# The second feed-forward's up products as seven block products, with weight sums made earlier and kept in DRAM

## The chip, the cores and the metric

The kernel runs on one core of one Trainium2 chip. The metric is the device time of one launch in microseconds (us), the median over runs. TensorE is called PE, its weight loads PEld, VectorE DVE, ScalarE ACT, GpSimd POOL and SyncE SP.

## The reference, cut to what matters

```python
for i in range(DEPTH):                       # two layers, 512 tokens, 256 more of context
    ...
    x = x + mods[2] * o_lat                  # layer 0: SSD and attention; layer 1: latent attention
    h = modulate(rmsnorm(x, norm2_g[i]), mods[3], mods[4])
    x = x + mods[5] * swiglu(h, ffn_w_up[i], ffn_w_down[i])
    ...
def swiglu(h, w_up, w_down):                 # w_up 1024 x 5632, w_down 2816 x 1024
    g, u = jnp.split(h @ w_up, 2, axis=-1)
    return (jax.nn.silu(g) * u) @ w_down
```

All of it is float32. In the second layer only the 512 tokens of x go through the feed-forward, in the first layer the 256 of the context too.

## The kernel before

**Numbers.** Every large product is made of three: each operand is split into a high part (rounded to fp32r) and a low part (the rest), and high x high, high x low and low x high are added up in PSUM. For a weight piece of 128 x 1024, `WStream.split` makes both parts: ACT copies the raw piece `wr` into `wh` (line 150), and POOL or DVE, by the string `W.pat`, subtracts to give `wl` (line 151). `W.lim(nraw, nhl)` sets how many raw pieces are loaded and how many split ahead; pieces come in a fixed order, and all DMAs are issued by SP's one queue (line 133 for weights).

**Stages.** The SSD and attention of layer 0 take the first 850 us or so, and then come the first feed-forward (`ffn(0, 6, ...)`, to some 1400 us), the latent attention (`mla_in`, `mla_attention`, to 1714 us), its output product with the norm of the feed-forward (`out_gemm` with `begin_norm`, to some 1787 us), the second feed-forward (`ffn(1, 4, ...)`) and the final norm. Beside the first feed-forward DVE also makes the modulation vectors (`acc`, line 409) from a stream `wa` of their own.

**A feed-forward.** The 2816 hidden columns are 11 pairs of 128-wide tiles; `FFN_PARTS` groups the pairs as 2, 3, 3, 3. Per pair there are four up pieces of 512 KB (gate and up, each in two halves of the 1024 inputs). `mm_w` (lines 662, 663, 665) keeps the weights still and moves the tokens: for each of 2 hidden tiles, gate and up, 8 input tiles and 3 forms it issues one matmul of 512 columns in the second feed-forward, 96 per pair. The first pair runs in two halves of 256 columns, so that it can begin before all tokens are normalized. `act` then makes `sg` = silu(gate) x up (ACT line 1272, DVE line 1273) and splits it into `hh` and `hl` (lines 499, 500). After each part `out_gemm` (lines 521 to 523) multiplies with the down pieces; one matmul chain per token tile and half of the outputs fills a PSUM bank `g`, of which there are two, DVE multiplies it with the gate (`gt`, line 1212), and POOL or DVE adds it to `x` (line 1213). A few steps of the next part's first up product are taken ahead of the down products.

**The attention.** 16 units, each of which ends with the row sums: DVE's reciprocal `rc`, POOL's copy `rb` (line 1068), two PE transposes, ACT's copy `rs`, DVE's product `oT`. POOL also adds the rotary parts of `q` (line 1446).

**Order.** The kernel is written as generators that are advanced side by side: `drive(main, side, ratio)` advances `side` by `ratio` steps for each step of `main`. The framework's scheduler then orders each engine's instructions once, before the run; on the chip every engine goes through its list in that order.

## Time and profile before

| | us |
|---|---|
| median of 3 runs | 2141.45 |
| lowest, highest | 2141.02, 2143.85 |
| the profiled execution | 2141.09 |
| its span | 2139.3 |

The page gives the span of one profiled execution and each engine's busy time in it; the remaining 1.8 us of its time lie around the span. Line numbers in rows are those of the kernel before. A row of a group gives busy time and mean duration of one instruction, then how long the engine had been idle just before them and what ended that. Matmuls are pipelined: their rows overlap, and the distance of two starts is what one costs.

### The profile page before, as it was taken

The page shows a single profiled execution, that of the slowest core. Times are in us where ns is not written, and L with a number is a line of the kernel's source. Part 1 is how long each engine was busy: PE and PEld are TensorE (multiplying, and loading weights), DVE is VectorE, ACT ScalarE, POOL GpSimd, SP SyncE. Part 2 cuts the span into 40 slices and gives each one's busy share as a digit, 9 for nine tenths or more (in the row PEclk, how much of TensorE's full clock was granted, in tenths as well). Part 3 has the DMA queues.
Part 4 walks back from the last instruction along what each step waited for, and adds up shares of the span by engine and source line. Part 5 has one row for each costly group of instructions (what it writes and reads, how often), then busy time and mean ns, then how long its engine had stood idle before and what let it go on. Part 6 is the DMA issues. An engine that isn't in the chain of part 4 may idle for free. (4 is left out here: it accounts for less than half of the span.)

```text
span 2139.3 us, 29481 instructions
## 1 busy us (share of the span) xinstructions
PE 2053.9 (96%) x11420; PEld 1690.0 (79%) x11420; DVE 1212.1 (57%) x2103; ACT 844.0 (39%) x1717; POOL 798.8 (37%) x701
## 2 busy tenths in 40 slices
PE   6999999999999899999999999999999999999998
PEld 3777777777777677888888878889888878888886
DVE  4689887867664697845345252175656663323223
ACT  4456544336664234312202212254655644222222
POOL 2456544584322355432222222254110154333333
PEclk9999999999999999999999999999999999999999
DMA  8211102510001641433335443112000033333232
GB/s 285 61 30 40 31 20 80 163 40 21 1 1 41 226 148 60 148 120 116 98 105 163 148 129 97 52 51 53 15 12 31 30 94 104 90 99 100 87 98 69
DMA packets 127573, 179.52 MB, mean 84 GB/s; under 512 B 16189, under 2 KB 77770, under 8 KB 127434
## 3 DMA queue, kind: packets, MB, share of 16 engines
q1 hardware_dynamic: 127434, 177.64, 26.4%
q8 instruction: 90, 1.47, 0.3%
q14 instruction: 49, 0.40, 0.1%
HBM read 172.35 MB, written 5.27 MB: 83 GB/s over the span
## 5 line engine op out<-in xcount | busy, mean ns | idle before, releaser
L151 POOL TENSOR_TENSOR wl<-wr,wh 128x1024 fp32r<-128x1024 f32 (+3 forms) x125 | 304.1, 2434 | 403.0 <-ACT wh L150 291.7
L150 ACT ACTIVATE wh<-wr 128x1024 fp32r<-128x1024 f32 (+3 forms) x211 | 218.6, 1038 | 520.0 <-DMA wr<-in_ffn_w_up_dram 135.5
L663 PE MATMUL gu<-hl,wh 128*128 128x512 f32 (+1 forms) x768 | 288.2, 376 | 1.5 <-POOL hl L500 1.5
L662 PE MATMUL gu<-hh,wh 128*128 128x512 f32 (+1 forms) x768 | 288.4, 376 | 0.0
L665 PE MATMUL gu<-hh,wl 128*128 128x512 f32 (+1 forms) x768 | 287.6, 375 | 0.0
L409 DVE SCALAR_TENSOR_TENSOR acc<-wa,sst,acc 128x512 f32<-128x512 f32 (+1 forms) x196 | 183.1, 977 | 89.1 <-DMA wa<-in_ada_w_dram 89.0
L151 DVE TENSOR_TENSOR wl<-wr,wh 128x1024 fp32r<-128x1024 f32 (+3 forms) x86 | 115.1, 1338 | 167.2 <-ACT wh L150 143.9
L521 PE MATMUL g<-wh,hh 128*128 128x512 f32 (+2 forms) x520 | 199.4, 384 | 0.5 <-DVE gt L1212 0.5
L522 PE MATMUL g<-wl,hh 128*128 128x512 f32 (+2 forms) x520 | 198.3, 381 | 0.0
L523 PE MATMUL g<-wh,hl 128*128 128x512 f32 (+2 forms) x520 | 197.4, 381 | 0.0
L1212 DVE TENSOR_TENSOR gt<-g,gate 128x512 f32<-128x512 f32 x132 | 90.5, 689 | 180.0 <-PE g L523 176.6
L662 PEld LDWEIGHTS gu<-hh,wh 128*128 128x128 f32 x768 | 144.4, 188 | 30.3 <-issue 2.9
L500 POOL TENSOR_TENSOR hl<-sg,hh 128x768 fp32r<-128x768 f32 (+1 forms) x44 | 71.8, 1632 | 247.0 <-ACT hh L499 246.9
L663 PEld LDWEIGHTS gu<-hl,wh 128*128 128x128 f32 x768 | 144.7, 188 | 16.6 <-POOL hl L500 1.7
L665 PEld LDWEIGHTS gu<-hh,wl 128*128 128x128 f32 x768 | 144.7, 189 | 15.6
L1052 DVE TENSOR_REDUCE nm<-S 128x1 f32<-128x768 f32 x128 | 122.1, 954 | 48.4 <-PE S L1512 27.6
L1213 POOL TENSOR_TENSOR x<-x,gt 128x512 f32<-128x512 f32 x66 | 89.6, 1362 | 131.6 <-DVE gt L1212 122.8
L248 PE MATMUL PTp<-ident,Pm 128*128 128x128 f32 x832 | 123.1, 276 | 6.5 <-ACT PT L1087 2.1
L1054 ACT ACTIVATE Pm<-S,nm 128x768 f32<-128x768 f32 x128 | 115.1, 899 | 25.2 <-DVE nm L1052 24.4
L248 PEld LDWEIGHTS PTp<-ident,Pm 128*128 128x128 f32 x832 | 96.0, 141 | 23.5 <-issue 9.2
L521 PEld LDWEIGHTS g<-wh,hh 128*128 128x128 f32 x520 | 97.6, 188 | 20.0 <-DVE gt L1212 1.0
L523 PEld LDWEIGHTS g<-wh,hl 128*128 128x128 f32 x520 | 97.7, 188 | 19.5
(311 smaller groups left out, 4687.2 us busy)
## 6 DMA issues: line engine op xcount, KB each, us to landing
wa<-in_ada_w_dram SPq DMA_DIRECT2D x96, 512.0 KB, 4.8
wr<-in_ffn_w_up_dram SPq DMA_DIRECT2D x88, 512.0 KB, 3.6
wr<-in_ffn_w_down_dram SPq DMA_DIRECT2D x44, 512.0 KB, 4.2
wr<-in_ab_w_in_dram SPq DMA_DIRECT2D x36, 512.0 KB, 3.8
wr<-in_ab_w_out_dram SPq DMA_DIRECT2D x16, 512.0 KB, 5.5
wr<-in_mla_w_o_dram SPq DMA_DIRECT2D x8, 512.0 KB, 3.6
yscr<-y SPq DMA_DIRECT2D x12, 256.0 KB, 3.7
yr<-yscr SPq DMA_DIRECT2D x6, 512.0 KB, 4.2
```

The lines of the kernel that those rows point to most:

```text
L150: nc.scalar.activation(hi, raw, AF.Copy)
L151: eng.tensor_tensor(lo, raw, r32(hi), op=ALU.subtract)
L248: self.nc.tensor.transpose(out, in_, self.ident[:n, :n])
L409: nc.vector.scalar_tensor_tensor(acc[:, v], in0=raw[:, kk], scalar=c, in1=acc[:, v], op0=ALU.mult, op1=ALU.add)
L521: nc.tensor.matmul(ps, h, wh[:, kk, :], start=(n == 0), stop=False)
L522: nc.tensor.matmul(ps, h, wl[:, kk, :], start=False, stop=False)
L523: nc.tensor.matmul(ps, l, wh[:, kk, :], start=False, stop=(n == nk - 1))
L662: nc.tensor.matmul(o, a, hi[:, c0:c1], start=st, stop=False)
L663: nc.tensor.matmul(o, a, lo[:, c0:c1], start=False, stop=False)
L665: nc.tensor.matmul(o, b, hi[:, c0:c1], start=False, stop=sp)
L1052: nc.vector.tensor_reduce(nm, sp[:, :, 0:w], axis=AX.XY, op=ALU.max, negate=True)
L1054: nc.scalar.activation(p[:, 0:nkt * P].rearrange("p (a b) -> p a b", a=2), sp[:, :, 0:w], AF.Exp, bias=nm, accum_out=x["sum"][:, ti, a:a + 1])
```

## The change

The feed-forward of layer 1 is rewritten for pairs 1 to 10. The tokens (two halves of 256) and the inputs (two halves of 512) cut the activations into four blocks `11`, `12`, `21`, `22`; the inputs, and gate and up, cut a pair's weights into four. The two-by-two block product, which takes eight block products, is made with seven, of which four use sums of weight blocks and four use sums of activation blocks (`S1` to `S4`). Each block product is 24 matmuls of 256 columns (`mm_q`). `up7` adds up the results out of PSUM: five sums on DVE, two copies on ACT, two sums on POOL, then Silu, products and splits.

The sums of weights are made by `sums_w`, four per block, from a second load of the weights (`wq`), and stored to a DRAM tile `w7` that the weight stream reads later: pairs 1 to 5 on DVE beside the first feed-forward (40 items of 128x128 blocks), pairs 6 to 10 on POOL beside the attention (20 items of 128x256). An item is two loads, four operations and one store. A pair takes seven pieces of 512 KB instead of four; four of them are read from `w7`. `begin_norm_q` keeps the normalized tokens (`hfT`), and `sums_q` makes the activation sums between the halves of the first pair, eight DVE operations and their splits. All of a part's hidden tiles of a pair come out of the last of its products; one product of the next part is taken ahead of the down products. In the attention and the output product all weight splits go to DVE, in the second feed-forward two of three (`VVP`); four raw pieces are loaded and five split ahead there. The modulation vectors of layer 1 get one or two steps more between their product and its use.

```diff
+SUMS_0, SUMS_1, SUMS_2 = 6, 0.16, 0.17
...
+def along(main, side, ratio, wait):
+    acc = -wait * ratio
+    for _ in main:
+        acc += ratio
+        while acc >= 1.0:
+            acc -= 1.0
+            next(side, None)
+        yield
+    for _ in side:
+        pass
...
             for j in pairs:
-                gs = bp(up, 0, KD, 256 * j, 256, 4)
-                self.i_up[l, j] = (pre + W.add(gs[len(pre):]), W.add(bp(up, 0, KD, HID + 256 * j, 256, 4)))
+                ops = self.up_pieces(l, j)
+                ids = pre + [W.add([s])[0] for s in ops[len(pre):]]
+                self.i_up[l, j] = (ids[:2], ids[2:]) if len(ids) == 4 else ids
...
+    def up_pieces(self, l, j):
+        up = self.a["ffn_w_up"][l]
+        g, u = (self.block_pieces(up, 0, KD, x + 256 * j, 256, 4) for x in (0, HID))
+        if l == 0 or j == 0:
+            return g + u
+        if j not in self.w7:
+            self.w7[j] = self.dp.tile([P, 4, 4, 256], F32, name=self.nm("w7"))
+        t = [self.w7[j][:, n] for n in range(4)]
+        return [g[0], t[1], t[0], g[1], t[3], t[2], u[1]]
+
+    def sums_w(self, pairs, w, V, alloc):
+        nc = self.nc
+        up = self.a["ffn_w_up"][1].rearrange("(s k p) (x f) -> k s p x f", s=2, p=P, x=2)
+        items = [(j, kt, c) for j in pairs for kt in range(4) for c in range(0, 256, w)]
+        def load(j, kt, c):
+            t = alloc([P, 2, 2, w], F32, "wq")
+            for s in range(2):
+                nc.sync.dma_start(t[:, s], up[kt, s][:, :, 256 * j + c:256 * j + c + w])
+            return t
+        ts = [load(*x) for x in items[:2]]
+        yield
+        for n, (j, kt, c) in enumerate(items):
+            t = ts.pop(0)
+            V.tensor_tensor(t[:, 0, 1], t[:, 1, 1], t[:, 0, 1], op=ALU.subtract)
+            V.tensor_tensor(t[:, 0, 0], t[:, 0, 0], t[:, 0, 1], op=ALU.add)
+            yield
+            V.tensor_tensor(t[:, 1, 0], t[:, 1, 0], t[:, 0, 0], op=ALU.subtract)
+            V.tensor_tensor(t[:, 1, 1], t[:, 1, 1], t[:, 0, 0], op=ALU.subtract)
+            yield
+            if n + 2 < len(items):
+                ts.append(load(*items[n + 2]))
+            nc.sync.dma_start(self.w7[j][:, :, kt, c:c + w], t.rearrange("p s x c -> p (s x) c"))
+            t = None
...
+    def split_q(self, src, name, tt, eng):
+        c = slice(tt * P, tt * P + P)
+        (h3, h1), (l3, l1) = self.q[name]
+        for h, lo, s in ((h3[:, :, c], l3[:, :, c], src[:, 0:3]), (h1[:, c], l1[:, c], src[:, 3])):
+            self.nc.scalar.activation(h, s, AF.Copy)
+            eng.tensor_tensor(lo, s, r32(h), op=ALU.subtract)
...
+    def sums_q(self):
+        V, G = self.nc.vector, self.nc.gpsimd
+        self.quarters(("S1", "S2", "S3"))
+        for tt in range(2):
+            h1, h2 = self.hf[tt], self.hf[2 + tt]
+            a11, a12, a21, a22 = h1[:, 0:4], h1[:, 4:8], h2[:, 0:4], h2[:, 4:8]
+            V.tensor_tensor(a22, a21, a22, op=ALU.add)
+            V.tensor_tensor(a21, a11, a21, op=ALU.subtract)
+            self.split_q(a21, "S3", tt, G)
+            V.tensor_tensor(a11, a22, a11, op=ALU.subtract)
+            self.split_q(a11, "S2", tt, V)
+            self.split_q(a22, "S1", tt, G)
+            V.tensor_tensor(a12, a12, a11, op=ALU.subtract)
+            self.split_q(a12, "S4", tt, V)
...
+    def mm_q(self, outs, i, name, start, stop):
...
+        for o, m0 in outs:
+            for kk in range(4):
...
+                nc.tensor.matmul(o, a, hi, start=st, stop=False)
+                nc.tensor.matmul(o, a, lo, start=False, stop=False)
+                nc.tensor.matmul(o, b, hi, start=False, stop=sp)
...
+    def up7(self, ids, hh, hl):
...
+            elif n == 2:
+                t["u2"] = two(self.med(512, "hf"))
+                V.tensor_tensor(t["u2"], ps, t["p1"], op=ALU.add)
+            elif n == 3:
+                sg = t["sg"] = self.e([P, 2, 2, 256], F32, "sg7")
+                V.tensor_tensor(sg[:, :, 0], ps, t.pop("p1"), op=ALU.add)
+                nc.scalar.activation(sg[:, :, 0], sg[:, :, 0], AF.Silu)
+            elif n == 4:
+                w, u2 = t["w"], t["u2"]
+                V.tensor_tensor(w[:, 0], ps, u2, op=ALU.add)
+                G.tensor_tensor(u2, u2, w[:, 1], op=ALU.add)
+                G.tensor_tensor(w[:, 1], w[:, 1], w[:, 0], op=ALU.add)
...
+        for n, name in enumerate(("11", "S3", "S2", "12", "S1", "22", "S4")):
...
+            yield from self.mm_q([(ps[:, m], m * P) for m in range(2)], ids[n], name, True, True)
+            self.W.free(ids[n])
+            ev(n, ps)
+            yield
...
-        drive(self.ffn(0, NT, LateGates(self, 0, 5, side), lambda: self.begin_norm(1, 0)), side, ADA_DVE)
+        drive(along(self.ffn(0, NT, LateGates(self, 0, 5, side), lambda: self.begin_norm(1, 0)),
+                    self.sums_w(range(1, SUMS_0), P, nc.vector, self.s), SUMS_1, 60), side, ADA_DVE)
...
-        drive(self.mla_attention())
+        W.pat = "V"
+        W.lim(2, 3)
+        drive(along(self.mla_attention(), self.sums_w(range(SUMS_0, 11), 256, nc.gpsimd, self.f), SUMS_2, 2))
...
-        drive(self.out_gemm(self.oh, self.ol, 4, self.i_mo[1], range(NL), gate, self.begin_norm(1, 3)))
+        W.lim(2, 4)
+        drive(self.out_gemm(self.oh, self.ol, 4, self.i_mo[1], range(NL), gate, self.begin_norm_q(1, 3)))
...
-        W.lim(1, 6)
+        W.pat = "VVP"
+        W.lim(4, 5)
         gate = [self.gate(1, 5, 0)]
-        drive(self.ffn(1, NL, gate, self.final))
+        drive(self.ffn_q(1, gate, self.final))
```

**The order, first place: POOL in the second attention.** Before, between two units' copies `rb`, stand rotary sums (`q`) or nothing:

```order
L1446 TENSOR_TENSOR q_13734<-q_13734,qp_13890 128x4x32
L1068 COPY rb_13929<-rc_13927 128x256
L1068 COPY rb_14054<-rc_14052 128x256
L1068 COPY rb_14180<-rc_14178 128x256
L151 TENSOR_TENSOR wl_14216<-wr_13878,wh_14215 128x768
L1068 COPY rb_14381<-rc_14379 128x256
```

With the change, the additions of the weight sums (`wq`) are among them:

```order
L1123 COPY rb_14100<-rc_14098 128x256
L1677 TENSOR_TENSOR q_14077<-q_14077,qp_14117 128x4x32
L636 TENSOR_TENSOR wq_14155<-wq_14155 128x256
L637 TENSOR_TENSOR wq_14155<-wq_14155 128x256
L1677 TENSOR_TENSOR q_14077<-q_14077,qp_14150 128x4x32
L639 TENSOR_TENSOR wq_14155<-wq_14155 128x256
L640 TENSOR_TENSOR wq_14155<-wq_14155 128x256
L1677 TENSOR_TENSOR q_14078<-q_14078,qp_14196 128x4x32
L1677 TENSOR_TENSOR q_14078<-q_14078,qp_14247 128x4x32
L1123 COPY rb_14292<-rc_14290 128x256
```

Every item puts four additions on POOL, and a weight split (`wl`) no longer stands there.

**Second place: DVE at the end of the first part of the first feed-forward.** Before, the gated products `gt` of the down product follow each other:

```order
L1273 TENSOR_TENSOR sg_9050<-sg_9050,gu_8919 128x512
L1276 TENSOR_TENSOR sg_9050<-sg_9050,gc_8920 128x256
L409 SCALAR_TENSOR_TENSOR acc_8927<-wa_9105,sst_76,acc_8927 128x512 x4
L1212 TENSOR_TENSOR gt_9100<-g_9087,gate_9101 128x512
L1212 TENSOR_TENSOR gt_9122<-g_9109,gate_9101 128x512
L1212 TENSOR_TENSOR gt_9140<-g_9125,gate_9101 128x512
```

Now eleven additions stand ahead of these rows and eight more between the first three products:

```order
L639 TENSOR_TENSOR wq_9279<-wq_9279 128x128
L1267 TENSOR_TENSOR gt_9158<-g_9145,gate_9159 128x512
L640 TENSOR_TENSOR wq_9279<-wq_9279 128x128
L1267 TENSOR_TENSOR gt_9182<-g_9167,gate_9159 128x512
L637 TENSOR_TENSOR wq_9348<-wq_9348 128x128
L639 TENSOR_TENSOR wq_9348<-wq_9348 128x128
L640 TENSOR_TENSOR wq_9348<-wq_9348 128x128
L636 TENSOR_TENSOR wq_9426<-wq_9426 128x128
L637 TENSOR_TENSOR wq_9426<-wq_9426 128x128
L639 TENSOR_TENSOR wq_9426<-wq_9426 128x128
L640 TENSOR_TENSOR wq_9426<-wq_9426 128x128
L1267 TENSOR_TENSOR gt_9200<-g_9185,gate_9159 128x512
```

At the ends of the second and third part the additions stand in the same way, up to 28 ahead of the third `gt`.

**Third place: DVE within a pair of the second feed-forward.** Before, a pair is two products `sg` and two weight splits:

```order
L1273 TENSOR_TENSOR sg_17182<-sg_17182,gu_17109 128x512
L151 TENSOR_TENSOR wl_17171<-wr_17144,wh_17170 128x1024
L1273 TENSOR_TENSOR sg_17238<-sg_17238,gu_17189 128x512
L151 TENSOR_TENSOR wl_17271<-wr_17180,wh_17270 128x1024
```

Now it is five sums out of PSUM (`gu`, `gc`), a product, a split `hl` and four or five weight splits:

```order
L1480 TENSOR_TENSOR hf_18236<-gu_18205,hf_18170 128x512
L165 TENSOR_TENSOR wl_18231<-wr_18093,wh_18230 128x1024
L1487 TENSOR_TENSOR w_18203<-gu_18271,hf_18236 128x512
L1483 TENSOR_TENSOR sg_18268<-gu_18205,hf_18170 128x2x256
L165 TENSOR_TENSOR wl_18297<-wr_18168,wh_18296 128x1024
L1492 TENSOR_TENSOR sg_18268<-gu_18271,hf_18236 128x2x256
L165 TENSOR_TENSOR wl_18330<-wr_18201,wh_18329 128x1024
L1497 TENSOR_TENSOR w_18203<-gc_18338,w_18203 128x512
L1498 TENSOR_TENSOR sg_18268<-sg_18268,w_18203 128x2x256
L516 TENSOR_TENSOR hl_18376<-sg_18268,hh_18375 128x512
```

The weight splits stand between the sums that free PSUM.

## Rows read from the trace of the kernel before

**Rows 1.** Page, part 1: busy time, share of the span, instructions by engine.
```profile
PE 2053.9 (96%) x11420; PEld 1690.0 (79%) x11420; DVE 1212.1 (57%) x2103; ACT 844.0 (39%) x1717; POOL 798.8 (37%) x701
```

**Rows 2.** Stretches: first feed-forward, attention, output product, second feed-forward.
```profile
core 0: us, PE busy (x) PEld busy (x) DVE busy (x) ACT busy (x) POOL busy (x), PEclk, DMA share, GB/s
850.00:1400.00 550.00, 546.21 (x3005) 463.30 (x3004) 247.95 (x342) 124.38 (x186) 164.84 (x97) 0.99 0.37 116
1490.00:1714.00 224.00, 216.30 (x1536) 189.58 (x1534) 141.50 (x234) 133.10 (x283) 26.86 (x38) 0.99 0.07 22
1714.00:1787.00 73.00, 71.16 (x417) 62.33 (x418) 45.11 (x85) 32.64 (x68) 37.32 (x35) 1.00 0.31 97
1787.00:2101.00 314.00, 314.00 (x1358) 254.69 (x1358) 83.12 (x86) 85.83 (x100) 111.85 (x62) 1.00 0.32 97
```

**Rows 3.** Waits of PE, 840 to 1400 us, then 1720 to 2140: total, times, longest.
```profile
PE ada L419 <- DVE acc L409: 2.7, 1, 2.7
...
PE gu L663 <- POOL hl L500: 1.5, 1, 1.5
```

**Rows 4.** Timeline of PE (92 matmuls, first and last) and of its weight loads.
```profile
1776.08 0.28 PE L662 MATMUL gu<-hh,wh 128*128 128x256 f32 x1
...
1786.83 0.28 PE L665 MATMUL gu<-hh,wl 128*128 128x256 f32 x1
...
1776.44 0.19 PEld L663 LDWEIGHTS gu<-hl,wh 128*128 128x128 f32 x1
1776.56 0.19 PEld L665 LDWEIGHTS gu<-hh,wl 128*128 128x128 f32 x1
```

**Rows 5.** Groups by form in the second feed-forward, 1787 to 2101 us.
```profile
L151 POOL TENSOR_TENSOR wl<-wr,wh 128x1024 fp32r<-128x1024 f32 x29 | 69.6, 2399 | 96.4 <-ACT wh L150 87.4 <-PE g L523 9.0
L150 ACT ACTIVATE wh<-wr 128x1024 fp32r<-128x1024 f32 x58 | 61.5, 1061 | 175.9 <-DMA wr<-in_ffn_w_up_dram 116.5 <-DMA wr<-in_ffn_w_down_dram 34.9 <-POOL wl L151 24.5
...
L151 DVE TENSOR_TENSOR wl<-wr,wh 128x1024 fp32r<-128x1024 f32 x29 | 41.9, 1444 | 77.4 <-ACT wh L150 64.4 <-PE gu L663 12.5 <-PE g L522 0.5
...
L1273 DVE TENSOR_TENSOR sg<-sg,gu 128x512 f32<-128x512 f32 x21 | 14.5, 688 | 80.2 <-ACT sg L1272 80.2
```

**Rows 6.** Line 151, the low split: ns min/median/max of DVE's.
```profile
L151 DVE TENSOR_TENSOR wl<-wr,wh x86: 559/1226/2343, 286.4 to 2097.6; 128x1024 fp32r<-128x1024 f32 x79, 128x768 fp32r<-128x768 f32 x4, 128x384 fp32r<-128x384 f32 x2, 128x864 fp32r<-128x864 f32 x1
```

**Rows 7.** Timeline, 1826 to 1830 us: start, length, engine.
```profile
1826.85 1.29 POOL L1213 TENSOR_TENSOR x<-x,gt 128x512 f32<-128x512 f32 x1 [5.61 <-DVE gt L1212]
...
1827.23 1.99 DVE L151 TENSOR_TENSOR wl<-wr,wh 128x1024 fp32r<-128x1024 f32 x1 [0.46 <-PE g L522]
...
1829.15 0.68 DVE L1212 TENSOR_TENSOR gt<-g,gate 128x512 f32<-128x512 f32 x1
```

**Rows 8.** DMA issues in the second feed-forward: count, KB, us to landing.
```profile
wr<-in_ffn_w_up_dram SPq DMA_DIRECT2D x35, 512.0 KB, 3.6
```

**Rows 9.** Groups by form of DVE in the first feed-forward.
```profile
L409 DVE SCALAR_TENSOR_TENSOR acc<-wa,sst,acc 128x1024 f32<-128x1024 f32 x28 | 37.1, 1323 | 53.1 <-DMA wa<-in_ada_w_dram 53.0
...
L500 DVE TENSOR_TENSOR hl<-hf,hh 128x128 fp32r<-128x128 f32 x17 | 7.1, 452 | 0.0
```

**Rows 10.** Waits of SP's queue, 840 to 1450 us: total, times, longest.
```profile
SPq L133 <- PE g L523: 168.9, 17, 47.5
```

**Rows 11.** Line 1164, a 128x256 subtraction on POOL: ns min/median/max.
```profile
L1164 POOL TENSOR_TENSOR ol<-of,oh x24: 725/737/1050, 509.6 to 692.4; 128x256 fp32r<-128x256 f32 x24
```

**Rows 12.** Tile rb in the second attention: first and last start.
```profile
L248 PE MATMUL O<-ident,rb x32: 270/272/299, 1518.5 to 1709.0; 128*128 128x128 f32 x32
L1068 POOL COPY rb<-rc x16: 397/402/407, 1504.4 to 1705.6; 128x256 f32<-128x256 f32 x16
```

**Rows 13.** Groups by form, 1714 to 1787 us: the weight splits.
```profile
L151 POOL TENSOR_TENSOR wl<-wr,wh 128x1024 fp32r<-128x1024 f32 x6 | 15.2, 2538 | 5.0 <-ACT wh L150 2.9 <-DVE wl L151 1.8 <-POOL hl L500 0.2
...
L151 DVE TENSOR_TENSOR wl<-wr,wh 128x1024 fp32r<-128x1024 f32 x6 | 7.3, 1220 | 8.8 <-PE gu L663 6.5 <-ACT wh L150 2.3
```

More of the change, by code (lines that the diff above doesn't have):

```diff
@@ new lines, in begin_norm_q, with norm, after @@
+    def begin_norm_q(self, l, ch):
+        nc = self.nc
+        self.q, self.hf = {}, [None] * NL
+        self.quarters(("11", "12", "22"))
+        self.quarters(("21", "S4"))
+        A, B = self.mod[l][:, ch + 1, 0, :], self.mod[l][:, ch, 0, :]
+        live = {}
+        def norm(xn, t):
+            hf = self.hf[t] = self.e([P, KD, P], F32, "hfT")
+            for h in range(2):
+                ps = self.ps("nT", [P, 4, P])
+                for i in range(4):
+                    kt = 4 * h + i
+                    self.tr(ps[:, i, :], xn[:, kt * P:(kt + 1) * P])
+                for i in range(4):
+                    kt = 4 * h + i
+                    nc.vector.tensor_scalar(hf[:, kt, :], ps[:, i, :], A[:, kt:kt + 1], B[:, kt:kt + 1], op0=ALU.mult, op1=ALU.add)
+                self.split_q(hf[:, 4 * h:4 * h + 4], f"{t // 2 + 1}{h + 1}", t % 2, nc.gpsimd if h else nc.vector)
+        def after(t, nb):
+            if nb == 0:
+                live[t] = self.f([P, D], F32, "xn"), self.small(2, "s2")
+            xn, s2 = live[t]
+            self.norm_half(self.x[t], xn, s2, nb)
+            if nb == 0:
+                return None
+            del live[t]
+            nc.scalar.activation(xn, self.x[t], AF.Copy, scale=self.rstd2(s2))
+            return lambda: norm(xn, t)
+        return after
```

96 lines of the change are left out of this document (91 added, 5 removed).

## The prediction

> **What bounds the kernel now.** I read the page first, then the stretches, then the waits of TensorE, then single rows. PE is busy 96% of the span [rows 1]. [...]
>
> **Term 1, the matmuls: minus 23.7 us.** A pair of hidden tiles (j = 1 to 10) now takes 96 matmuls of 512 columns; the change makes seven products of 24 matmuls of 256 columns, 168 in all. The 512-column step is 314.00 / 1358 = 0.2312 us [rows 2]. The 256-column step stands in the first pair, which already runs in halves: from 1776.08 to 1786.83 us there are 92 matmuls, so 10.75 / 91 = 0.118 us [rows 4]. That is a little over half of 0.2312, so halving the columns loses only some 2%. Per pair: 96 x 0.2312 = 22.20 us against 168 x 0.118 = 19.82 us, 2.37 us less; ten pairs give 23.7 us. The first pair keeps its 192 matmuls of 256 columns, and the down products are unchanged.
>
> A narrow matmul could be held up by its own weights: each step loads a new 128x128 block, one load is 0.19 us in the rows, longer than the 0.118 us step, and loads too start every 0.12 us [rows 4]. They overlap, so the step above is already the price with a load each time. [...]
>
> **Term 2, engines beside the second feed-forward: plus 5 us.** Per pair the weight pieces go from four to seven. Each costs ACT 1.06 us, then POOL 2.40 us or DVE 1.23 us undisturbed [rows 5, 6]. By the pattern VVP that is 4.67 x 1.23 = 5.7 us on DVE, 2.33 x 2.40 = 5.6 us on POOL and 7.4 us on ACT. The seven products add five DVE sums out of PSUM at 0.69 us (the price of the sg product [rows 5]), 3.4 us, and on DVE a multiply and a split with both inputs in SBUF, 0.69 us each, 1.4 us; POOL gets two sums, a product and one split at some 1.3 us (its 128x512 sum takes 1.29 [rows 7]), 5.2 us; ACT two copies, two Silus and two splits at about 0.6 us, 3.7 us. Sums: DVE 10.5, POOL 10.8, ACT 11.1 us, each under 19.8 us.
>
> What speaks against adding these up apart: DVE and POOL disturb each other. A DVE split takes 1226 ns in the median and up to 2343; one that starts at 1827.23 us, inside a POOL sum that ends at 1828.14 us, takes 1.99 us, about what it has to wait plus its usual time, while the DVE product from PSUM beside the next POOL work keeps its length [rows 5 to 7]. If DVE's 7.1 us of two-SBUF-input work and POOL's 10.8 us exclude each other, that is 17.9 us of 19.8 us per pair: it fits with 10% to spare. If every POOL instruction fully delays DVE, DVE needs 10.5 + 10.8 = 21.3 us, 1.5 us too much per pair. Bounds for ten pairs: 0 and 15 us; I take 4, nearer the lower end, because five pieces are split ahead (four products, 11 us of PE work) and DVE's PSUM sums can run beside POOL. [...]
>
> The last product of a part leaves a DVE sum, a DVE multiply, two ACT splits and two low splits before the down products: 0.69 + 0.69 + 1.3 + 1.3 = 4.0 us. PE has the first 12 down matmuls (2.8 us) and, except in the last part, one product taken ahead (2.8 us) as cover: 0 to 1.2 us at the last, 1 us taken.
>
> Traffic is no term: seven pieces of 0.52 MB in 19.8 us are 185 GB/s against 97 GB/s now at a 0.32 share of the DMA engines [rows 2], so about 0.6, and a piece lands in 3.6 us [rows 8] where it is loaded four ahead.
>
> **Term 3, the sums in the first feed-forward: plus 2 us.** DVE gets 160 additions of 128x128 beside 248 us of work in 550 us [rows 2]. A DVE operation of that shape with two SBUF inputs is 452 ns here, contention included [rows 9], so about 72 us; from the 0.69 us of four times the columns at least 28 us. DVE goes to 60% at most. What matters is who stands behind them: in the order, 20 to 28 additions stand ahead of the third gated product (gt) of each of three parts, and a late gt holds one of two PSUM banks of the down products. PE takes 12 x 0.231 = 2.8 us per bank in the first part, 18 x 0.231 = 4.2 us later. At 452 ns 20 additions (first part) are 9.0 us and 28 are 12.7 us; three banks of cover are 8.3 and 12.5 us. So 0 to 1 us per part if the loads have landed; 2 us taken, from 0 to 10.
>
> On SP the sums issue 80 loads and 40 stores in the same queue as the weights, and a store heads the queue until DVE has done its four additions. The queue has room: it waits 168.9 us for PE to release buffers [rows 10], so the weights are ahead of their use.
>
> **Term 4, the sums in the second attention: plus 1.5 us.** POOL gets 80 additions of 128x256 at 737 ns [rows 11], 59 us beside 27 us of work in 224 us [rows 2]. Behind them on POOL stand the 16 copies rb, on which each unit's last step hangs. Between two of them the order shows four to eight additions, so a copy may come up to 5.9 us later. In the trace the first copy is at 1504.4 and its product on PE at 1518.5 us, the last 3.3 us ahead at 1705.6 and 1709.0 us [rows 12]: mostly slack. Bounds 0 and 8 us.
>
> **Term 5, between attention and second feed-forward: plus 2.5 us.** From 1714 to 1787 us POOL made six weight splits (15.2 us) and DVE six (7.3 us) [rows 13]; now DVE makes all of the output product's, beside 45 us of work in 73 [rows 2]. The activation sums add eight DVE operations of 0.69 us or more, and splits on DVE and POOL; they are due one after the other over the first pair's second half and the next products, some 16 to 30 us. Bounds 0 and 8 us; PE waited 1.5 us here before.
>
> **The sum.** 2141.09 us (the profiled execution, 0.36 us under the median of the runs) - 23.7 + 4 + 1 + 2 + 1.5 + 2.5 = 2128.4 us. I forecast **2128.5 us**.
>
> **The rivals.**
> - *All covered.* Every added operation hides: 2141.1 - 23.7 = 2117.4 us. For it: PE has next to no waits anywhere now [rows 3], with the same kind of stream. Against: four places where a margin is only some microseconds.
> - *DVE and POOL saturate.* Each POOL instruction delays DVE in full, 15 us in term 2 instead of 4: 2139.4 us, no measurable change. For it: the 1.99 us row; against: DVE's PSUM sums need no turn. [...]
> - *Late products in the first feed-forward (slower).* The additions wait for their own loads: DVE goes through two items in a burst, and if one landing of 3.6 us [rows 8] is open for every two of six items, 10.8 us come on top of, say, 24 x 0.452 = 10.8 us. The third gt is then some 10 us late, in three parts 30 us: 2128.4 + 28 = 2156 us. It decides as soon as loads are issued behind stores that wait; below about 3 us of lateness per part nothing shows. Against: DVE waits 53 us for the loads of one form of acc in this stretch [rows 9], and PE does not notice.
> - *Weights not overlapped.* If each 256-column step took the 0.19 us of its load [rows 4], a pair would take 168 x 0.19 = 31.9 us, 9.7 more than now: 97 us for ten pairs, 2238 us. Against: the 92 matmuls at 0.118 us. [...]
> - *The change does not do what it says.* Were the sums not finished in their stages, a block of them would stand before the next stage. The order has the last four of DVE's in the last part's first pair and the last of POOL's ahead of the last o splits, so I give this no share.
>
> **How the numbers follow.** Between runs of this kernel 0.2% (4.3 us) is about what can be told from no change. Forecast 0.58 (2121 to 2137 us), all covered 0.16, saturated 0.12, late products 0.10, weights 0.01, something not listed on the slower side 0.03. Faster: the first two and a sixth of the saturated case, 0.76; the same: the rest of the saturated and a little of the late case, 0.11; slower 0.13. The range runs from 2117 us, the covered case, to 2144 us, past the saturated case and into the first of the late one; some 0.15 is left out. The forecast's own range is 2121 to 2137 us.
>
> **What would show it.** Right: matmuls of the second feed-forward at 0.118 us, its stretch about 20 us shorter, PE's waits there a few microseconds on DVE and POOL splits. Term 2 is wrong if PE waits for wl pieces in every pair, with DVE splits near 2 us. Term 3 is wrong if PE waits for gt between 860 and 1390 us, term 4 if it waits for rs in attention. The forecast falls if the 256-column step is not 0.118 us, or if the stretches before 1714 us grow by more than 10 us.

## The result, and the profile after

The change takes **2121.25 us** (median of 5 runs, 2119.75 to 2125.81) against 2142.07 us for the kernel before in the same comparison: a ratio of 0.9907, with an interval of 0.9893 to 0.9921. That is 20 us less, 17 to 23 by the interval; forecast were 2128.5 us, 12.6 us less than the profiled execution of before. The profiled execution of the change took 2120.97 us, its span 2119.2 us. Medians and ratios here and below are over the runs in the faster state, which leaves out one of the four runs of e3 (7582.58 us).

The page's first part, to be held against [rows 1], and three stretches, to be held against [rows 2] (same columns; the last is cut to where the change's own stage lies):

```profile
PE 2036.3 (96%) x12140; PEld 1710.1 (81%) x12140; DVE 1369.5 (65%) x2361; ACT 890.5 (42%) x1770; POOL 886.6 (42%) x791
```

```profile
850.00:1400.00 550.00, 544.86 (x2977) 459.49 (x2976) 291.21 (x492) 122.95 (x181) 161.78 (x95) 0.99 0.48 151
1490.00:1712.00 222.00, 217.10 (x1537) 190.15 (x1536) 143.89 (x237) 134.63 (x284) 74.94 (x113) 0.98 0.37 115
1788.00:2078.00 290.00, 286.85 (x2041) 269.02 (x2040) 173.28 (x169) 125.76 (x152) 152.70 (x82) 0.99 0.50 155
```

PE has 720 instructions more and 17.6 us less work. In the second feed-forward it made 1358 matmuls in 314 us; now 2041 in 290. DVE has there 173 us of work in 290, POOL 153, ACT 126: the busy share of DVE has more than doubled, and PE still has 99%.

To see where the 20 us lie, the span is cut at the first and last starts of three kinds of matmul: the scores `S` of the second attention, the last form of the output product (`ol`) and of the down products (`hl`). First the kernel before, then the change (ns min/median/max, first and last start, forms):

```profile
L1510 PE MATMUL S<-kb,mQ x128: 331/340/522, 1490.8 to 1701.8; 96*128 96x384 f32 x128
...
L523 PE MATMUL g<-wh,ol x160: 387/393/628, 677.5 to 1760.5; 128*128 128x512 f32 x160
...
L523 PE MATMUL g<-wh,hl x520: 292/392/405, 932.8 to 2131.1; 128*128 128x512 f32 x147, 128*128 128x288 f32 x16, 128*128 128x384 f32 x11
```

```profile
L1741 PE MATMUL S<-kb,mQ x128: 333/338/446, 1491.3 to 1700.5; 96*128 96x384 f32 x128
...
L539 PE MATMUL g<-wh,ol x160: 387/394/628, 671.1 to 1758.9; 128*128 128x512 f32 x160
...
L539 PE MATMUL g<-wh,hl x520: 292/394/501, 929.9 to 2111.1; 128*128 128x512 f32 x147, 128*128 128x288 f32 x16, 128*128 128x384 f32 x11
```

The differences of these starts, for the two and for the kernels of the experiments (us; "attention" is from the first to the last `S`, "output" from there to the last `ol`, "second FFN" from there to the last `hl`):

| | to the first S | attention | output | second FFN | rest | span |
|---|---|---|---|---|---|---|
| before | 1490.8 | 211.0 | 58.7 | 370.6 | 8.2 | 2139.3 |
| the change | 1491.3 | 209.2 | 58.4 | 352.2 | 8.1 | 2119.2 |
| e1 products alone | 1487.7 | 202.9 | 58.5 | 352.0 | 8.1 | 2109.2 |
| e2 sums alone | 1489.4 | 209.3 | 58.8 | 371.6 | 7.9 | 2137.0 |
| e3 first bank | 1493.4 | 209.0 | 58.4 | 351.6 | 8.1 | 2120.5 |
| e4 pattern VP | 1493.8 | 209.6 | 58.4 | 353.6 | 8.1 | 2123.5 |
| e5 before, three ahead | 1488.2 | 203.8 | 58.7 | 370.5 | 8.2 | 2129.4 |
| e6 before, splits on DVE | 1488.9 | 210.0 | 58.7 | 370.5 | 9.1 | 2137.2 |
| e7 own buffers | 1488.5 | 203.9 | 58.5 | 352.5 | 8.1 | 2111.5 |
| e8 all splits on POOL | 1491.5 | 209.9 | 58.4 | 393.6 | 8.1 | 2161.5 |
| e9 buffers and bank | 1490.8 | 205.5 | 58.4 | 351.7 | 8.1 | 2114.5 |
| e10 all sums on DVE | 1515.4 | 203.1 | 58.4 | 350.8 | 8.2 | 2135.9 |
| e11 all sums on POOL | 1490.6 | 236.3 | 58.4 | 350.7 | 8.2 | 2144.2 |
| e12 three edits | 1492.2 | 205.5 | 58.4 | 351.5 | 8.1 | 2115.7 |

Two things stand in the first two lines. The second feed-forward gives 18.4 us, not the 23.7 of the matmuls alone. And the attention, where the change adds 59 us of POOL work, is 1.8 us *shorter*. The first column moves by 5 us between kernels that do the same work there (1488.5 in e7, 1493.8 in e4), so a few microseconds of any one execution are not the change's. The attention column holds such a piece too: in most executions the granted clock drops as the attention begins (to a mean of 0.96 over 40 us in e9, against 1.00 in e7), in e1, e5, e7, e10 and e11 it does not, and that is worth 1.6 us (the last section has the rows). The medians and their intervals carry the totals, the stages carry the reasons.

What PE waits for in the change (total, times, longest), first in the first feed-forward, then in the attention, then from the output product to the end:

```profile
PE g L537 <- DVE gt L1267: 1.7, 3, 0.9
...
PE PTp L262 <- DVE PT L1140: 1.9, 1, 1.9
...
PE g L1695 <- ACT PT L1142: 0.4, 1, 0.4
...
PE gu L1458 <- DVE sg L1540: 3.1, 1, 3.1
PE gu L1459 <- DVE q L1396: 0.6, 1, 0.6
```

Against [rows 3], and the same wait of the kernel before,

```profile
PE g L521 <- DVE gt L1212: 0.5, 1, 0.5
```

there is one new wait of 3.1 us at the entry of the second feed-forward, there are waits for `gt` in the first feed-forward of 1.7 us instead of 0.5, and two for `PT` in the attention. After 1794 us PE waits for nothing at all.

### The profile page after: what moved, and what is told of

Its sections match the earlier page's. It is cut to its first block, busy times and chain, and to the rows that moved or that the text cites. A ratio compares the mean times of both kernels' runs of the same rounds, so it can differ in the third digit from the quotient of the medians.

```text
span 2119.2 us, 31924 instructions
## 1 busy us (share of the span) xinstructions
PE 2036.3 (96%) x12140; PEld 1710.1 (81%) x12140; DVE 1369.5 (65%) x2361; ACT 890.5 (42%) x1770; POOL 886.6 (42%) x791
## 4 chain that ended last, share of the span: by engine, by line
PE 75%; DVE 12%; DMA 4%; ACT 4%; issue 3%; POOL 2%; SPq 0%; POOLq 0%; DVEq 0%; ACTq 0%
PE g L537 9%; PE g L538 8%; PE g L539 8%; PE O L1154 4%; PE PTp L262 4%; PE gu L717 3%; PE gu L718 3%; PE gu L720 3%; DVE acc L423 3%; PE gu L1459 2%; PE gu L1458 2%; PE gu L1460 2%; PE S L1223 2%; DMA wa<-in_ada_w_dram 2%; PE gc L720 2%
## 5 line engine op out<-in xcount | busy, mean ns | idle before, releaser
L164 ACT ACTIVATE wh<-wr 128x1024 fp32r<-128x1024 f32 (+3 forms) x241 | 250.0, 1040 | 483.1 <-PE g L538 181.9
L165 POOL TENSOR_TENSOR wl<-wr,wh 128x1024 fp32r<-128x1024 f32 (+2 forms) x115 | 286.0, 2488 | 361.7 <-ACT wh L164 233.3
L165 DVE TENSOR_TENSOR wl<-wr,wh 128x1024 fp32r<-128x1024 f32 (+3 forms) x126 | 174.6, 1386 | 79.3 <-ACT wh L164 65.0
L717 PE MATMUL gu<-hh,wh 128*128 128x512 f32 (+1 forms) x384 | 145.1, 378 | 0.0
L718 PE MATMUL gu<-hl,wh 128*128 128x512 f32 (+1 forms) x384 | 144.9, 377 | 0.0
L720 PE MATMUL gu<-hh,wl 128*128 128x512 f32 (+1 forms) x384 | 144.6, 377 | 0.0
L516 POOL TENSOR_TENSOR hl<-sg,hh 128x768 fp32r<-128x768 f32 (+1 forms) x34 | 62.4, 1837 | 165.3 <-ACT hh L515 152.4
L538 PEld LDWEIGHTS g<-wl,hh 128*128 128x128 f32 x520 | 98.5, 189 | 17.9
L537 PE MATMUL g<-wh,h1h 128*128 128x512 f32 x240 | 97.7, 408 | 3.9 <-DVE zt L968 3.9
L718 PE MATMUL gc<-hl,wh 128*128 128x256 f32 x352 | 99.0, 281 | 0.0
```

The lines of the kernel that those rows point to most:

```text
L164: nc.scalar.activation(hi, raw, AF.Copy)
L165: eng.tensor_tensor(lo, raw, r32(hi), op=ALU.subtract)
L537: nc.tensor.matmul(ps, h, wh[:, kk, :], start=(n == 0), stop=False)
L538: nc.tensor.matmul(ps, h, wl[:, kk, :], start=False, stop=False)
L717: nc.tensor.matmul(o, a, hi[:, c0:c1], start=st, stop=False)
L718: nc.tensor.matmul(o, a, lo[:, c0:c1], start=False, stop=False)
```

## The experiments

Ratios are to the kernel before on the same chip, with 95% intervals. Most intervals are 0.3% (6 us) wide, so single-microsecond questions are answered by the stage table and the waits.

**Which part costs, which gains: the products alone, the sums alone.** e1 reads all seven pieces of a pair from the weights and makes no sums:

```diff
-        if j not in self.w7:
-            self.w7[j] = self.dp.tile([P, 4, 4, 256], F32, name=self.nm("w7"))
-        t = [self.w7[j][:, n] for n in range(4)]
+        t = g + u
...
-        drive(along(self.mla_attention(), self.sums_w(range(SUMS_0, 11), 256, nc.gpsimd, self.f), SUMS_2, 2))
+        drive(self.mla_attention())
```

> Left out: the weight sums (their loads, additions and stores); the four pieces of a pair that were read from the sums' tile are read from the weights themselves, so that traffic, splits, products and activation sums are those of the change. By the prediction the sums cost 2 us in the first feed-forward and 1.5 us in the attention: this kernel is then 3.5 us faster than the change, near 2118. If the sums are covered (the trace of the change shows PE waiting 1.7 us for gt in the first feed-forward and next to nothing for POOL in the attention), it lies within 1.5 us of the change, 2119.5 to 2121. If the late products were at work after all, it gains 10 us or more.

Measured: 2113.0 us, 0.9867 (0.9853 to 0.9881), 28.5 us less than before. Against the change's 0.9907 the sums cost 0.40%, 8.6 us (the two intervals allow 3 to 15): more than the forecast's 3.5. The table puts 6.3 us of it in the attention (202.9 against 209.2; 4.7 without the clock drop at its start) and 3.6 ahead of it, which is within what that column moves by anyway. And it shows something that none of the expectations had: without sums the attention is 8.1 us shorter than *before*, 6.5 without the clock drop. Whatever that is, it is part of the change, and it isn't the products.

e2 is the other half, the sums with the old second feed-forward (`up_pieces` returns `g + u` for all pairs, `begin_norm` and `ffn` as before):

> The sums are made and stored as in the change, with the attention's splits on DVE, but the second feed-forward is the one of before and does not read them. By the prediction: 3.5 us over before, near 2145.5. If the sums are covered: within 2 us of before, 2142 to 2144. If late gated products cost as the slower rival has it: 15 to 28 us over before, 2157 to 2170.

Measured: 2138.15 us, 0.9984 (0.9975 to 0.9993), 3.4 us less than before: a kernel with 240 more additions, 120 loads and 60 stores that isn't slower at all. The late gated products as a heavy cost are out at this size. That it is faster points again to the attention (209.3 against 211.0).

**The hidden gain: three pieces split ahead.** With the sums the change sets `W.pat = "V"` and `W.lim(2, 3)` for the attention; before it was `PV` and `lim(2, 2)`. e5 is the kernel before with the limit alone, e6 with the pattern alone:

```diff
+        W.lim(2, 3)
         drive(self.mla_attention())
```

> The kernel before with one edit: in the second attention three weight pieces are split ahead instead of two, still in turn on POOL and DVE; no sums, the old second feed-forward. The ledger of the traces gives the change 6.3 us there which the prediction's sum does not hold: PE's five waits for the query weights' splits (4.7 us by rows, with the slower restart behind them) are gone. If it is the number split ahead: those waits vanish here, 5 to 6.5 us faster than before, near 2135. If it is the engine (DVE in place of POOL): no change here, 2140 to 2141.

> The kernel before with the other half of that edit: in the second attention all weight splits on DVE, still two ahead. If the number split ahead is the cause: PE's waits for wh stay (3.4 us) and only those for POOL's wl (1.3 us) go, 0 to 2 us faster, 2138.5 to 2140.5. If the engine is the cause: 5 to 6.5 us faster, near 2135.

Measured: e5 2133.48 us, 0.9973 (0.9963 to 0.9983); e6 2138.26 us, 0.9998 (0.9988 to 1.0008). The limit does it, 5.8 us by the ratio, 7.2 by the table (203.8 against 211.0), or 5.6 without the clock drop, which stands ahead of the first of these waits (in the kernel before the mean granted clock is 0.83 from 1490 to 1500 us, and the first wait for `wh` ends at 1507.30) and so is not the limit's; the engine does nothing that can be told from no change. PE's waits in the attention, of the kernel before and of e6 (same columns as above):

```profile
PE g L521 <- ACT wh L150: 3.4, 3, 1.2
PE g L522 <- POOL wl L151: 1.3, 2, 0.6
```

```profile
PE g L521 <- ACT wh L150: 3.4, 3, 1.2
```

The three waits for `wh` stay in e6 and are gone in e5 and in the change. They are the first of the query weights (`cqT` products), split too late because only two split pieces may live at a time; ACT makes the copy in 0.51 us once the place is free, then POOL the low part in 1.0 us, and PE stands there. So one line of the change, which does not belong to the seven products, is worth about a quarter of what they are. A kernel with that line alone is the right one to compare the products with: by ratio 2133.5 to 2121.25 is 12 to 14 us, not 20.

**What the sums cost in the attention: buffers, not work.** In the change ACT, DVE and PE come to a stop once, around 1632 us. The timeline of the change (start, length, engine, and in brackets the idle time before it and what ended it):

```profile
1628.01 0.56 SPq L644 DMA_DIRECT2D w<-wq  x1
...
1631.90 0.60 ACT L1142 ACTIVATE PT<-PTp 128x512 f32<-128x512 f32 x1 [3.80 <-DMA w<-wq]
1632.39 1.05 ACT L164 ACTIVATE wh<-wr 128x1024 fp32r<-128x1024 f32 x1
...
1632.55 0.44 PE L1695 MATMUL g<-cvT,wh 128*128 128x384 f32 x1 [0.42 <-ACT PT L1142]
...
1633.48 1.64 DVE L165 TENSOR_TENSOR wl<-wr,wh 128x1024 fp32r<-128x1024 f32 x1 [3.16 <-ACT wh L164]
...
1635.03 0.68 DVE L1140 COPY PT<-PTp 128x512 f32<-128x512 f32 x1
```

The store of a finished item is issued at 1628.01; ACT's copy `PT` has waited 3.80 us for it to land. `PT` and the sums' tiles `wq` come from one pool of 14 buffers, so the next `PT` takes over a buffer that a sum still holds. Behind ACT's copy, in its fixed order, stands the split `wh`; DVE waits 3.16 us for that, its own copy `PT` is late, PE waits 0.42 and 1.90 us. e7 gives the sums tiles from the pool that holds the residual `x`:

```diff
-        drive(along(self.mla_attention(), self.sums_w(range(SUMS_0, 11), 256, nc.gpsimd, self.f), SUMS_2, 2))
+        drive(along(self.mla_attention(), self.sums_w(range(SUMS_0, 11), 256, nc.gpsimd, self.e), SUMS_2, 2))
```

> The change with one edit: the second attention's weight sums take their tiles from the pool of the residual x, not from the one that also holds the copies PT and the weight pieces. In the change's trace ACT stands 3.80 us at a copy PT until a store of the sums has landed, DVE's next weight split waits 3.16 us for ACT, and PE waits 0.4 and 1.9 us for PT; a clock drop of 3.4 us follows. If the shared buffers are the cause: those waits are gone, 2.5 to 4.5 us faster than the change, 2116 to 2118. If it is POOL's additions as such (59 us of work, the prediction's reason), nothing changes, 2120 to 2121.5.

Measured: 2117.99 us, 0.9899 (0.9882 to 0.9915); the interval overlaps the change's, the stage is clearer: the attention goes from 209.2 to 203.9 us, 1.0 above e1, which makes no sums there. Of these 5.3 us, 1.6 are the clock drop at its start; e9 and e12, which have the same attention and the drop, take 205.5 us. So the buffers are worth some 3.7 us. POOL does the same 80 additions. PE's waits for `PT` in e7:

```profile
PE PTp L262 <- DVE PT L1140: 0.7, 2, 0.4
```

**How far each engine's slack goes.** e10 puts all sums on DVE (`SUMS_0, SUMS_1 = 11, 0.32`), e11 all on POOL (`SUMS_0, SUMS_2 = 1, 0.34`, with e7's pool).

> All ten pairs' weight sums on DVE beside the first feed-forward, 320 additions of 291 ns (93 us) at twice the rate, none on POOL. Up to 56 additions then stand ahead of a third gt: 16.3 us against 12.5 us of cover. If the late gated product is only off in size (the slower rival's mechanism): 3.8 us in each of three parts, 11 us more in the first feed-forward, less 4.5 us gained in the attention: near 2127. If the additions keep to DVE's idle time: 1.2 us of gt waits become 2 to 3, the attention gains 2.8 to 4.5: 2117 to 2119.

> All ten pairs' weight sums on POOL in the second attention, 160 additions of 731 ns (117 us beside 27 in 222), with tiles from the pool of x, none on DVE. If POOL's work is idle-time work once the buffers are its own: the first feed-forward gains 2.6 us over the run with own buffers and the attention loses under 1 us: 2115 to 2117. If the additions ahead of the copies rb begin to tell (up to 16 of 0.73 us, 11.7 us, against the 3.3 us of slack at the last copy): 8 us for the last units, 2124 or more; the sums' loads (40 of 0.26 MB more) are then also behind the weights on SP.

Measured: e10 2139.34 us, 1.0008 (0.9997 to 1.0020); e11 2144.64 us, 1.0029 (1.0019 to 1.0040). Each loses the whole gain. In e10 the stretch up to the first `S` is 24 us longer than in the change, and PE's waits between 840 and 1440 us say where it starts:

```profile
PE g L537 <- DVE gt L1267: 10.2, 7, 4.1
...
PE ada L433 <- DVE gt L1267: 1.9, 1, 1.9
PE g L538 <- DVE wl L165: 1.8, 1, 1.8
```

The `gt` waits, 1.7 us in the change, are 10.2 us, with 1.9 more where a modulation product follows, and splits and `hh` behind them. The expectation of 11 us for that mechanism had its size for these waits. From 840 us to the first `S` all of PE's waits together are some 17 us longer than in the change; the rest of the 24 us is not taken apart here. So the slower rival is real; the change stays below the load at which it costs much, by a factor of less than two.

e11 fell neither way that was written down: the attention is 27 us longer than in the change, and what PE waits for is not the copies `rb`. Its waits between 1480 and 1740 us, of PE, then of ACT and DVE:

```profile
PE PTp L262 <- DVE mQ L1723: 18.3, 3, 7.7
...
ACT mQ L1722 <- DMA w<-wq: 26.2, 5, 9.6
...
DVE mQ L1723 <- DMA w<-wq: 15.8, 2, 11.2
```

ACT and DVE wait 26.2 and 15.8 us for stores of sums before they may write `mQ`, which comes from the pool of `x` too. By the trace that is e7's mechanism again, in the other pool: at twice the rate of items the stores hold more buffers than are free. No run gives these sums more buffers, so this is read from the waits and not tested. Whether POOL itself has room for all sums isn't shown by this run.

**Whether POOL and DVE get in each other's way.** In the second feed-forward every other split on POOL (e4, `"VP"`), and all of them (e8, `"P"`):

> In the second feed-forward every other weight split goes to POOL instead of every third. Per pair of 19.84 us POOL then has 3.5 x 2.40 + 5.2 = 13.6 us and DVE 3.5 x 1.23 + 4.8 = 9.1 us by undisturbed durations. If each POOL instruction delays DVE in full (the saturated rival), DVE needs 22.7 us a pair: 2.9 us more than PE, some 29 us over the change, 2150. If only DVE's instructions with two SBUF inputs exclude POOL (5.7 us of the 9.1), 19.3 us: it just fits, 0 to 8 us slower, 2121 to 2129. If the two engines hardly disturb each other: no change, 2120 to 2122.

> In the second feed-forward all weight splits on POOL: 7 x 2.40 + 5.2 = 22.0 us of POOL work per pair of 19.84 us by undisturbed durations. If POOL's sum alone decides: 2.2 us over PE in each of ten pairs, some 22 us over the change, 2142, less what is made up during the down products (five pieces ahead, at most 3 parts x 5 x 2.4 us). If DVE's instructions with two SBUF inputs also hold POOL (1.4 us a pair): 2150 to 2156. If the work ahead covers it: 2121 to 2126.

Measured: e4 2123.37 us, 0.9916 (0.9902 to 0.9929); e8 2164.16 us, 1.0128 (1.0103 to 1.0153). e4 lies in the range of the middle theory and 26 us below full delay; its interval overlaps the change's, so it does not tell the middle theory from no disturbance. e8 is past the point where POOL alone decides. Its second feed-forward (same columns as the stretches above):

```profile
1788.00:2078.00 290.00, 267.27 (x1795) 244.81 (x1794) 100.32 (x100) 111.00 (x132) 245.32 (x124) 0.96 0.44 136
```

POOL is at 245 of 290 us there, PE at a granted clock of 0.96, and the stage takes 41.4 us more than in the change, above every expectation. PE's waits from 1788 us on come to 29.7 us, against 3.1 in the change, and most of the rest fits the lower granted clock (an estimate from the 0.96 of this row: 4% of a stage of some 330 us is 13 us).

In the change itself the same two engines show who delays whom. Groups by form between 1788 and 2078 us:

```profile
L165 DVE TENSOR_TENSOR wl<-wr,wh 128x1024 fp32r<-128x1024 f32 x58 | 89.7, 1547 | 32.1 <-ACT wh L164 25.5 <-POOL wl L165 6.4
...
L1489 POOL TENSOR_TENSOR w<-w 128x512 f32<-128x512 f32 x10 | 19.0, 1902 | 0.5
...
L1498 DVE TENSOR_TENSOR sg<-sg,w 128x512 f32<-128x512 f32 x9 | 8.1, 901 | 0.5
...
L1480 DVE TENSOR_TENSOR hf<-gu,hf 128x512 f32<-128x512 f32 x10 | 6.9, 689 | 8.7 <-PE gu L1460 8.7
```

DVE's sums out of PSUM (line 1480 and four more, one input in PSUM, one in SBUF) keep 689 ns; the one that starts at 1804.10 us takes 0.69 us inside a POOL sum that runs from 1803.17 to 1805.33. What has both inputs in SBUF is stretched: the product of line 1498, of the same size, to 901 ns, the low split to 1547 from 1226 undisturbed [rows 6]; of POOL's sums, 1.29 us undisturbed [rows 7], the one at line 1488 keeps 1289 ns and the one at line 1489 takes 1902. In these rows, of DVE's work only what has both inputs in SBUF gets longer beside POOL's. So the sum to go by was the smaller one of term 2, 17.9 of 19.8 us, and not that of the saturated rival; and it fitted.

**The entry of the second feed-forward.** The timeline of the change around PE's 3.1 us wait:

```profile
1788.22 2.47 POOL L165 TENSOR_TENSOR wl<-wr,wh 128x1024 fp32r<-128x1024 f32 x1 [1.47 <-ACT wh L164]
...
1788.36 2.75 DVE L1396 TENSOR_TENSOR qS<-hfT,qS 128x384 fp32r<-128x384 f32 x1
...
1790.17 1.28 ACT L1539 ACT_TABLE_LOAD   x1
...
1791.23 0.55 DVE L1396 TENSOR_TENSOR qS<-hfT,qS 128x384 fp32r<-128x384 f32 x1
...
1791.91 1.22 DVE L165 TENSOR_TENSOR wl<-wr,wh 128x1024 fp32r<-128x1024 f32 x1
...
1793.04 0.68 DVE L1540 TENSOR_TENSOR sg<-sg,gu 128x512 f32<-128x512 f32 x1
...
1793.77 0.58 PE L1458 MATMUL gu<-qS,wh 128*128 128x256 f32 x1 [3.15 <-DVE sg L1540]
```

PE ends the first pair's matmuls at 1787.6 us and one product of 24 later needs a bank `gu`. That bank is free when the first pair's gated product `sg` has read it; ahead of `sg` stand on ACT a table load of 1.28 us, on DVE an activation split that takes 2.75 us beside POOL's weight split, and a weight split. The 2.75 us are a row of two engines excluding each other: POOL's split runs from 1788.22 to 1790.69 us, and the next DVE split of the same form, begun after it, takes 0.55. The expectations of e3 and e12 call the long split S4's; by the order of DVE's list it is S2's, S4's sum stands ahead of it (0.68 us at 1787.76) and S4's own two pieces, 0.55 and 0.28 us, behind it. In the program's text e3 moves S4 behind `sg` and the table load forward:

```diff
-            V.tensor_tensor(a12, a12, a11, op=ALU.subtract)
-            self.split_q(a12, "S4", tt, V)
+            if tt:
+                self.nc.scalar.activation(self.small(1, "ex"), a21[:, 0, 0:1], AF.Silu)
...
+                    self.sums_q4()
```

> Two moves at the entry of the second feed-forward: the activation sum S4 and its split come after the first pair's gated products, and a one-element Silu after the split of S3 brings the table load forward. The change's trace has one wait there of 3.1 us, S2's product for a PSUM bank which the first pair's gated product holds, with a 1.28 us table load and a 2.75 us DVE split of S4 ahead of that product. If these two are the cause, the wait falls under 1 us and the time by about 3 us, with the clock drop that follows the wait by up to 5: 2116 to 2118.5. If the bank is late because of the weight splits in the two queues, the wait stays at 2 to 3 us and the time within 1 us of the change.

Measured: 2119.15 us, 0.9896 (0.9879 to 0.9913). The wait goes from 3.1 to 2.2 us:

```profile
PE gu L1467 <- DVE sg L1549: 2.2, 1, 2.2
```

On the chip the move happened only in part. The table load is ahead of the wait now, but on DVE the scheduler left S4's second sum (line 1453) and its small split ahead of `sg`, which starts at 1794.04:

```profile
1788.94 0.95 DVE L1453 TENSOR_TENSOR hfT<-hfT 128x512 f32<-128x512 f32 x1
...
1790.28 2.70 DVE L1396 TENSOR_TENSOR qc<-hfT,qc 128x128 fp32r<-128x128 f32 x2
```

The second row is one small split of S2 and one of S4; only S4's two large splits moved, to 1798.26 and 1800.28 us, and a weight split still stands ahead of `sg`. So e3 does not test a queue without S4. e9 takes away the need for the bank instead (`first and n == 2` gets a bank `g`, on top of e7):

```diff
-            if n in (0, 1, 6):
+            if n in (0, 1, 6) or first and n == 2:
```

> The kernel of the run with the sums' own buffers, and one more edit: in the first pair of seven products the second one after the overlap (S2) goes to a free bank g instead of a bank gu that the first pair's gated product still holds; 24 matmuls (2.8 us) later the bank gu is due. If the late bank is all of that 3.1 us wait: it falls to 0.3 us or less, and the clock drop that follows goes or stays by itself: 3 to 4.8 us faster than the run with own buffers alone, 2113 to 2115. If DVE, which holds S2's sum behind the same gated product, hands the wait on to the next product: 0 to 1 us, 2117 to 2118.

Measured: 2117.19 us, 0.9898 (0.9883 to 0.9914). The bank's wait is gone, and others are there:

```profile
PE gc L1458 <- ACT wh L164: 1.3, 1, 1.3
...
PE g L1459 <- DVE qS L1396: 0.4, 1, 0.4
PE g L537 <- ACT hh L515: 0.4, 1, 0.4
PE gc L1460 <- POOL wl L165: 0.3, 1, 0.3
```

2.4 us of waits in place of 3.1, in the products after it, for weight splits, an S split and `hh`: DVE and ACT are simply behind by then, as the second expectation had it. e12 puts all three edits together:

> The three edits that helped in their stretch put together: the attention's sums in buffers of the pool of x, S2's first product in a bank g, and S4's sums after the first pair's gated products with the Silu table load brought forward. The run with the first two still has 2.4 us of waits at the entry (1.3 for a weight's high part on ACT, 0.4, 0.3 and 0.4 for splits on DVE, POOL and ACT), behind a 1.28 us table load and S4's 2.76 us split. If these two hold the queues up: under 1 us of waits left there, 1.5 us faster, 2115.5 to 2116. If the weight splits themselves are late: waits of 2 us stay, 2117.

Measured: 2117.01 us, 0.9902 (0.9882 to 0.9921), with the same 1.3 us wait for `wh`. The time and the waits are those of the second expectation, that the queues are late and not one operation in them; as in e3, only S4's large splits moved, so it is not shown for S4 as a whole. e7, e9 and e12 have the lowest medians of the kernels that leave nothing out, 2117 to 2118 us; their intervals overlap the change's, so a gain of 1 to 4 us over it is likely and not proven.

## Why the prediction was right, point by point

- **Direction, range, size.** Faster, inside 2117 to 2144; 7 us better than the forecast. That is the net of a gain left out and three terms off in size. Without the gain the terms as measured would come to some 2127 us, close to the forecast, and that is partly luck: 5 us too much in term 2 make up for what terms 4 and 5 and the down products cost beyond the forecast.
- **Term 1, minus 23.7 us: right.** In the change one pair goes from 1854.44 to 1874.28 us, 19.84 us (forecast 19.82), and the next as long:

```profile
1854.44 0.28 PE L1458 MATMUL gc<-qS,wh 128*128 128x256 f32 x1
...
1874.28 0.28 PE L1458 MATMUL gc<-qS,wh 128*128 128x256 f32 x1
```

  Against 22.20 that is 2.36 us, 23.6 for ten. PE was busy for all of the 314.00 us of the old stretch [rows 2] and for 286.85 of 290 us of the new one, so the stage got shorter with its matmuls. Matmuls of 256 columns go at the 0.118 us that the first pair had shown, with a new weight block of 128x128 each time, whose load takes 0.19 us (a median of 187 to 188 ns at line 1459). So the rival of weights that do not overlap is out here (a load and a matmul one after the other would be more than the 0.19 us of that rival); e1 has the same pace, 352.0 us for the stage.
- **Term 2, plus 5 us: too much, it is 0.** The step that failed took 4 us for DVE and POOL in each other's way. PE has no wait at all after 1794 us. The sum of the work that excludes itself, 17.9 of 19.8 us, was the bound that held. The row that the step took for a DVE product beside POOL work (1829.15 us in [rows 7]) shows nothing of the kind: POOL is idle in that trace from 1828.14 to 1829.90 us. The 689 ns above are the row that does. The 1 us at the ends of parts is not there either. e4 and e8 show how near the edge is: one split in six moved to POOL costs some 2 us by the ratios (the intervals overlap), all of them 47.
- **Term 3, plus 2 us: right in kind, 1.2 us in waits for `gt`.** An addition took 291 ns in the median and 348 in the mean, not 452. That was the mean of 17 in which some were stretched; the median of all 64 of that line and shape in the trace of before is 294:

```profile
L636 DVE TENSOR_TENSOR wq<-wq x40: 277/291/2165, 831.8 to 1300.5; 128x128 f32<-128x128 f32 x40
```

  That lateness sets in steeply is shown by e10.
- **Term 4, plus 1.5 us: the size was within its bounds, the place was wrong.** The step looked at who stands behind the additions on POOL (`rb`); those never were late enough. The cost, some 3.7 us by e7 and e9, came from the buffers: the copies `PT` on ACT and DVE had to wait for the sums' stores to land. The question "who waits for that" was asked of POOL's queue and not of the tiles' pool.
- **Term 5, plus 2.5 us: near, 3.7 us of waits against 1.5 before,** and a stretch of lower granted clock behind it (0.57 from 1793 to 1797 us). The forecast named late splits and activation sums; what PE waits for is a PSUM bank that `sg` still has to read, behind just those operations.
- **What the sum left out: minus 6 us in the attention.** The section on the change had `W.lim(2, 3)` in its diff, and the step that went through the change priced the pattern `V` next to it and not the limit. Before, PE waited 3.4 us for `wh` and 1.5 for `wl` there; [rows 3] stopped at the first and the second feed-forward, and so the waits were not on the list of what could go. With it, and with the terms as measured, the sum is: matmuls minus 23.6, three ahead minus 5.6 (e5), buffers plus 3.7 (e7 and e9), entry plus 2.2, `gt` plus 1.2: minus 22.1, against minus 20.1 between the spans. Against the other 2 us stand 1.4 of a drop of the clock (below) and an estimated 1.3 of the down products: 0.2339 us a step in the last part of the change and 0.2315 before (33.45 and 33.10 us for 143 steps), 0.0024 for each of 528 steps if the other parts are like the last; why is open. The account closes to about a microsecond.
- **The rivals.** *All covered* (2117.4) was nearer than the forecast, but not because all was covered: in e1, with no sums, the time is 4 us under it. *Saturated*, every POOL instruction delaying DVE in full, is out: e4 is 26 us below it, and DVE's sums out of PSUM keep their length. What e8 runs into is POOL's own 22.0 us a pair. *Late products* is what e10 leads to, a mechanism of this kernel above the load that the change puts on.

## What to carry to other kernels

Go through a diff line by line for limits and patterns of prefetching as for operations, and list PE's waits in every stage that a line touches: here a line beside the products was worth 6 of the 20 us. Work put into an engine's idle time costs little as work (59 us of additions on POOL made e7's attention 1.0 us longer than e1's); ask which tiles it holds, for how long (until its store has landed), and who gets those buffers next. And slack is not linear: half the sums on each engine cost a few microseconds, all of them on DVE cost the whole gain; all on POOL did too, there by the buffers that the stores held.

## What the runs showed of the hardware that was not expected

The granted clock fell to 0.57 after two short stops of PE in the change. The two stretches, each with the one before it (columns as above, PEclk near the end):

```profile
1632.00:1636.00 4.00, 1.67 (x9) 1.23 (x9) 2.52 (x5) 3.23 (x7) 2.55 (x3) 1.00 0.18 60
1636.00:1640.00 4.00, 4.00 (x24) 2.26 (x24) 2.12 (x5) 2.08 (x4) 2.35 (x5) 0.57 0.39 121
1789.00:1793.00 4.00, 1.62 (x14) 1.41 (x12) 4.00 (x5) 3.97 (x5) 1.70 (x1) 1.00 0.00 0
1793.00:1797.00 4.00, 3.23 (x16) 3.23 (x17) 2.54 (x4) 3.07 (x6) 2.54 (x2) 0.57 0.54 182
```

In both, PE had work for 1.6 to 1.7 of 4 us, and in the next 4 us the mean granted clock was 0.57. The 48 matmuls that start at 1793.77 take 7.07 us where the 48 of a later pair, from 1857.27, take 5.66: such a drop adds 1.4 us to a wait of 3.1. It does not always follow: e10 and e11 have the wait of 3.0 and 3.2 us at the entry, and their mean granted clock from 1790 to 2078 us is 1.00, where the change has 0.99.

Chance shows best where two kernels do the same. In e7 and e9 the attention is the same code, and just before and at the first `S` PE waits 0.3, 0.6 and 0.3 us in both. First e9, then e7:

```profile
1490.00:1530.00 40.00, 38.79 (x251) 36.20 (x251) 27.91 (x48) 25.52 (x54) 18.60 (x26) 0.96 0.41 125
```

```profile
1490.00:1530.00 40.00, 39.63 (x279) 36.68 (x279) 28.08 (x49) 26.89 (x57) 18.23 (x26) 1.00 0.45 138
```

The clock fell in e9 (0.96) and not in e7, and the attention takes 205.5 and 203.9 us. Before, the change, e2, e3, e4, e6, e8, e9 and e12 have this drop, e1, e5, e7, e10 and e11 do not: of the 48 matmuls `gv` with the low weights (128x256), some of which stand at the attention's start, the longest takes 415 to 419 ns in the former and 284 or 285 ns in the latter. So a stage's time is compared only after its granted clock has been looked at.
